# A first MLP group of four tiles with the mean-square work inside it, and the MLP's operands rounded under the output projection's last column

## The chip, the core and the metric

The kernel runs on one core of one Trainium2 chip. The metric is the device time of one execution in microseconds (us), and what is compared is the median of several executions. Each execution of the profile is one run recorded by the hardware profiler. Engines go by short names in rows: PE is TensorE (matmuls; PEld is its weight load), DVE is VectorE, ACT is ScalarE, POOL is GpSimd, SP is the engine that issues most of the transfers, and SPq its queue of transfers.

## What is computed

The program is one step of a decoder layer for a prompt of 1024 tokens and 8 x 4 sample tokens (1056 in all) at a model width of 1024. An input projection feeds three branches (sparse attention, a state space model, attention into a memory), whose gated outputs are joined to 1536 columns. The change lies behind these, in the last three steps:

```python
def merge(x, o_a, o_b, o_c, gb, w_o):
    mixed = jnp.concatenate([o_a, o_b, o_c], axis=-1) * gb
    return x + mixed @ w_o                       # 1056 x 1536 by 1536 x 1024
def ffn(x, g, w1, w2):
    h = rmsnorm(x, g)                            # mean square over 1024, + 1e-6
    return x + jnp.square(jax.nn.relu(h @ w1)) @ w2    # 1024 -> 4096 -> 1024
# and a last rmsnorm(x, final_norm_g)
```

## The kernel before

**Products.** Everything is float32, and a product of two float32 operands is made as three matmuls in TensorE's rounded type fp32r. Each operand is split into its rounded value (`hi`) and the remainder (`lo`), and `mm3` (lines 122 to 124) adds hi x hi, hi x lo and lo x hi into one bank. `split` (line 112 for the rounding, line 118 for the remainder) rounds on ScalarE and subtracts on GpSimd, or on VectorE where it is called with "dve". The tokens are held in three chunks of 352 columns, so a matmul is 128 x 128 weights by 128 x 352.

**Output projection** (`out_proj`). The 1024 outputs are 8 columns `m` of 128. For each column and each of the three chunks, 12 operand tiles `k` are added up: 108 matmuls. The weights of a column come in two halves, `k` 4 to 11 and `k` 0 to 3; the last column takes `k` 0 to 3 first. `residual(m)` loads the rows of `x_prompt` and `x_sample` for the column into a tile `xr` of its own, transposes them on TensorE and lets ScalarE copy them into `acc`. `add` adds the column's three banks to `acc` on VectorE, and squares the sum on ScalarE (tile `sq`), which VectorE adds into the running sum of squares `ms` (its rows read `msb`).

**MLP** (`ffn`). First the operand `h` is split: 24 pieces (8 of the width by 3 chunks), each as `h2hi` on ScalarE (line 1704) and `h2lo` on VectorE (line 1705), scaled by the norm's weight alone. The root of the mean square is left out here: the squared ReLU lets it be taken out of the whole MLP, so `acc` is multiplied by the mean square instead, and the last norm puts that right with `rm`, its reciprocal. The 4096 hidden columns are 32 tiles of 128, in groups. Per tile: weights `w_ff1` (load into one of three `raw` buffers, split into `hi`, `lo`), 72 matmuls, then per chunk a ReLU (ScalarE, tile `rl`, line 1735), a square (VectorE, 1736), a rounding `yh` (ScalarE, 1737) and a remainder `yl` (VectorE, 1738); and the load and split of the tile's second-layer weights `w_ff2` (line 1742, `f2hi` on ScalarE and `f2lo` on GpSimd). After a group, its second layer: for each of 8 outputs and 3 chunks, three matmuls per tile, and one VectorE add into `acc` (line 1761). Before, the groups are 14 of two tiles and one of four.

**The mean square.** After the first group's first layer, `scale_acc` sums `ms` over the partitions with a matmul by ones for each chunk (line 1713), scales the sums on VectorE (`msb`, line 1714) and multiplies the 8 pieces of `acc` by them, four on VectorE and four on GpSimd (line 1717). Behind it TensorE transposes `ms` (line 1752), and VectorE takes the reciprocals `rm` (line 1753). All of this stands ahead of the group's second layer, whose adds go to the scaled `acc`.

**What sets the order.** The program is written against a framework that schedules it: pools give out buffers (a fourth `raw` has to wait for the first's last reader), and each engine's queue is put in order when the program is built, by an estimate of when instructions can start. At run time each engine goes through its queue strictly in order. So a row can stand in another place of a queue than in the source.

## Time and profile before

| what | value |
|---|---|
| median of three runs | 2028.8 us (2024.67 to 2034.67) |
| the profiled execution's own time | 2028.2 us |
| its span, from first to last instruction | 2026.4 us |
| mean granted clock of TensorE over the span | 0.967 |
| TensorE busy | 94% of the span |
| VectorE, ScalarE, GpSimd busy | 57%, 37%, 21% |

The profiled execution lies within the range of the three runs. TensorE is busy nearly throughout, so what other engines do shows in the time only where TensorE waits for them, or where it runs at a lower granted clock (1.00 in a table by stretch is its full level). A timeline row gives the start, the duration (for several instructions the time from the first's start to the last's end), the instruction as output tile <- input tiles, and in brackets how long the engine was idle before it and what ended that.

### The profile page before, as it was taken

Reading aid. Unit: us, or ns where it says so; the run is one execution under the profiler, and the core shown is the slowest. Engines: PE = TensorE matmul, PEld = TensorE weight load, DVE = VectorE, ACT = ScalarE, POOL = GpSimd, SP = SyncE. Lnnn points to the kernel's source line nnn. Section 1 sums busy time; section 2 is a strip of 40 time slices with the busy share of each in tenths; the row PEclk is TensorE's granted clock in tenths of the full one; section 3 lists DMA queues with packets and bytes.
Section 4 is the critical chain, followed back from the end, with each engine's and each line's share of the span. In section 5 each row is a group of like instructions: output and inputs, shape, how many; then the busy total and the mean of one; then the engine's idle time right before and its main releaser. Section 6 shows DMA issues by size and latency. Waiting matters only on the chain.

```text
span 2026.4 us, 33851 instructions
## 1 busy us (share of the span) xinstructions
PE 1912.8 (94%) x13280; PEld 1727.5 (85%) x13280; DVE 1154.9 (57%) x2759; ACT 756.7 (37%) x1696; POOL 434.4 (21%) x281
## 2 busy tenths in 40 slices
PE   8998999999997999999987999799999999999997
PEld 8987889999996665656545999799999999999997
DVE  6387995425536777787653225745554555554535
ACT  6301224226645676667643224122222211122222
POOL 2043431441112211011100122422211211122200
PEclk9998999999997899999996999899999999999999
DMA  7453334563345533232226222211111111111102
GB/s 266 147 138 87 99 92 111 177 214 126 126 129 143 160 96 117 84 106 71 90 93 190 74 70 62 62 51 44 53 53 42 46 49 43 42 43 52 42 1 86
DMA packets 197609, 191.44 MB, mean 94 GB/s; under 512 B 32845, under 2 KB 176966, under 8 KB 196234
## 3 DMA queue, kind: packets, MB, share of 16 engines
q1 hardware_dynamic: 190730, 154.13, 25.5%
q0 software_dynamic: 6720, 35.16, 5.1%
q8 instruction: 104, 1.70, 0.4%
q14 instruction: 55, 0.45, 0.1%
HBM read 155.34 MB, written 38.55 MB: 96 GB/s over the span
## 4 chain that ended last, share of the span: by engine, by line
PE 51%; DMA 2%; DVE 2%; issue 1%; ACT 1%; SPq 0%; DVEq 0%; POOL 0%; ACTq 0%; POOLq 0%
PE fps L122 12%; PE fps L124 12%; PE fps L123 12%; PE ops L122 2%; PE ops L123 2%; PE ops L124 2%; PE O L903 2%; PE T L889 2%; DMA xs<-cache_slc_kv,idx 1%; PE S L838 1%; PE S L835 1%; PE sS L1494 1%; DMA raw<-w_o 1%; DVE acc L1717 0%; PE xps L1651 0%
## 5 line engine op out<-in xcount | busy, mean ns | idle before, releaser
L1761 DVE TENSOR_TENSOR acc<-fps,acc 128x352 f32<-128x352 f32 (+3 forms) x360 | 185.1, 522 | 156.5 <-PE fps L124 156.5
L123 PE MATMUL fps<-h2lo,hi 128*128 128x352 f32 x768 | 248.6, 324 | 2.0 <-DVE h2lo L1705 2.0
L122 PE MATMUL fps<-h2hi,hi 128*128 128x352 f32 x768 | 248.2, 324 | 1.9 <-ACT h2hi L1704 1.9
L123 PE MATMUL fps<-yl,f2hi 128*128 128x352 f32 (+3 forms) x768 | 246.3, 323 | 3.3 <-DVE yl L1738 3.3
L124 PE MATMUL fps<-h2hi,lo 128*128 128x352 f32 x768 | 249.1, 324 | 0.0
L122 PE MATMUL fps<-yh,f2hi 128*128 128x352 f32 (+3 forms) x768 | 242.6, 325 | 6.0 <-DVE rm L1753 6.0
L124 PE MATMUL fps<-yh,f2lo 128*128 128x352 f32 (+3 forms) x768 | 245.9, 323 | 0.0
L1736 DVE TENSOR_TENSOR rl<-rl 128x352 f32<-128x352 f32 x96 | 132.2, 1378 | 146.1 <-ACT rl L1735 146.1
L118 POOL TENSOR_TENSOR lo<-raw,hi 128x1024 fp32r<-128x1024 f32 (+1 forms) x43 | 96.8, 2252 | 359.1 <-ACT hi L112 359.1
L124 PE MATMUL pso<-hhi,wlo 128*128 128x352 f32 x480 | 157.3, 328 | 0.0
L123 PE MATMUL pso<-hlo,whi 128*128 128x352 f32 x480 | 157.3, 328 | 0.0
L122 PE MATMUL pso<-hhi,whi 128*128 128x352 f32 x480 | 157.2, 328 | 0.0
L118 POOL TENSOR_TENSOR f2lo<-raw,f2hi 128x1024 fp32r<-128x1024 f32 x32 | 79.1, 2474 | 361.6 <-ACT f2hi L112 348.5
L843 DVE TENSOR_REDUCE nst<-S 128x1 f32<-128x384 f32 (+4 forms) x264 | 108.9, 433 | 80.2 <-PE S L838 59.5
L122 PEld LDWEIGHTS fps<-yh,f2hi 128*128 128x128 f32 x768 | 144.0, 189 | 7.8 <-DVE rm L1753 6.3
L123 PEld LDWEIGHTS fps<-yl,f2hi 128*128 128x128 f32 x768 | 144.8, 189 | 5.0 <-DVE yl L1738 3.6
L123 PEld LDWEIGHTS fps<-h2lo,hi 128*128 128x128 f32 x768 | 145.4, 189 | 2.3 <-DVE h2lo L1705 2.3
L122 PEld LDWEIGHTS fps<-h2hi,hi 128*128 128x128 f32 x768 | 145.2, 189 | 2.2 <-ACT h2hi L1704 2.2
L124 PEld LDWEIGHTS fps<-h2hi,lo 128*128 128x128 f32 x768 | 146.1, 190 | 0.0
L124 PEld LDWEIGHTS fps<-yh,f2lo 128*128 128x128 f32 x768 | 144.8, 189 | 1.4
L844 ACT ACTIVATE P<-S,nst 128x384 f32<-128x384 f32 (+4 forms) x264 | 127.4, 489 | 33.3 <-DVE nst L843 29.1
L112 ACT ACTIVATE f2hi<-raw 128x1024 fp32r<-128x1024 f32 x32 | 33.8, 1059 | 282.6 <-PE fps L123 268.7
(593 smaller groups left out, 4535.5 us busy)
## 6 DMA issues: line engine op xcount, KB each, us to landing
raw<-w_ff SPq DMA_DIRECT2D x64, 512.0 KB
wraw<-w_in SPq DMA_DIRECT2D x28, 512.0 KB
xs<-cache_mem_kv SPq DMA_DIRECT2D x16, 512.0 KB
s_gb<-st SPq DMA_DIRECT2D x36, 176.0 KB
x<-x_prompt SPq DMA_DIRECT2D x8, 512.0 KB
wraw<-w_mem_kv SPq DMA_DIRECT2D x8, 512.0 KB
qd<-s_q SPq DMA_DIRECT2D x32, 128.0 KB
ngb<-s_gb SPq DMA_DIRECT2D x64, 64.0 KB
```

What stands on the lines that cost most here:

```text
L112: nc.scalar.activation(hi, src, AF.Copy)
L118: eng.tensor_tensor(lo, src, hi.bitcast(F32), op=ALU.subtract)
L122: mm(ps, ahi, bhi, start=start, stop=False)
L123: mm(ps, ahi, blo, start=False, stop=False)
L124: mm(ps, alo, bhi, start=False, stop=stop)
L835: nc.tensor.matmul(S[:, :w], ctx["QA"][:, qs], KA[:, k0:k0 + w], start=True, stop=False)
L843: nc.vector.tensor_reduce(t[:, 0, pi, i:i + 1], S[:, o:o + pw], axis=AX.X, op=ALU.max, negate=True)
L844: nc.scalar.activation(P[:, o:o + pw], S[:, o:o + pw], AF.Exp, bias=t[:, 0, pi, i:i + 1], accum_out=t[:, 1, pi, i:i + 1])
L889: nc.tensor.transpose(T[:w, i * 128:(i + 1) * 128], Ps[i, si][:, o:o + w], self.ident)
L903: nc.tensor.matmul(O[c * 64:(c + 1) * 64, :256], v, pv[:w, c], start=n == 0, stop=n == total - 1)
L1736: tt(r, r, r, op=ALU.mult)
L1761: tt(acc[:, m, o:o + n], ps[:, :n], acc[:, m, o:o + n], op=ALU.add)
```

## The change

Four things are changed.

1. The first group has four tiles (0 to 3) instead of two; the two-tile groups begin at tile 4, and the last four stay.
2. The sums over the partitions, the transposes, the reciprocals and the scaling of `acc` are called after tile 1 of the first group, and tiles 2 and 3 follow.
3. The split of `h` for the widths 0 to 6 (all but the last) is called within the last column of the output projection, after its first half; the pool with the first half's operands (`mixb`) is closed there, and `h2hi` and chunk 0 of `h2lo` are laid into its space. For chunks 1 and 2 only `h2hi` is called there.
4. The residual's rows go into the `raw` buffers and into `rl` instead of a tile of their own, and the squares into `rl`.

```diff
-GROUPS = [(2 * i, 2) for i in range(14)] + [(28, 4)]
+GROUPS = [(0, 4)] + [(2 * i, 2) for i in range(2, 14)] + [(28, 4)]
...
-        with self.pool("acc") as rp, self.pool("wts") as wp:
-            with self.pool("mixb") as pool, self.pool("wop", PSUM) as psp:
+        with self.pool("acc") as rp, self.pool("wts") as wp, ExitStack() as self.fst:
+            with self.pool("wop", PSUM) as psp:
+                mb = ExitStack()
+                pool = mb.enter_context(self.pool("mixb"))
                 self.split(*self.mix_tiles(pool, range(4)), self.mixs[:, 0:4], e_lo="dve")
-                self.out_proj(rp, wp, pool, psp)
+                self.out_proj(rp, wp, pool, psp, mb)
...
         def residual(m):
-            xr = pool.tile([128, 9, 128], F32, name="xr", tag="xr", bufs=1)
-            nc.sync.dma_start(xr[:, 0:8], A["x_prompt"][0][:, cols(m)].rearrange("(i p) c -> p i c", p=128))
-            nc.sync.dma_start(xr[:NS, 8], xsv[:, cols(m)])
+            xr = wp.tile([128, 8, 128], F32, name="raw", tag="raw", bufs=3)
+            nc.sync.dma_start(xr, A["x_prompt"][0][:, cols(m)].rearrange("(i p) c -> p i c", p=128))
+            xrs = rp.tile([128, 512], F32, name="rl", tag="rl", bufs=2)
+            nc.sync.dma_start(xrs[:NS, 0:128], xsv[:, cols(m)])
             for i0 in (0, 4, 8):
                 pt = bank()
                 for i in range(i0, min(i0 + 4, 9)):
                     r = 128 if i < 8 else NS
-                    nc.tensor.transpose(pt[:, (i - i0) * 128:(i - i0) * 128 + r], xr[:r, i], self.ident[:r, :r])
+                    nc.tensor.transpose(pt[:, (i - i0) * 128:(i - i0) * 128 + r], xr[:, i] if i < 8 else xrs[:r, 0:128], self.ident[:r, :r])
...
-                    sq = pool.tile([128, 352], F32, name="sq", tag="sq", bufs=2)
+                    sq = rp.tile([128, 512], F32, name="rl", tag="rl", bufs=2)[:, :n]
...
+                if m == KT - 1 and ks[0] == 0:
+
+                    mb.close()
+                    fh = self.fst.enter_context(self.pool("ffh"))
+                    self.h2hi = fh.tile([128, KT, NT], R32, name="h2hi")
+                    self.h2lo = [fh.tile([128, KT, CHUNKS[0][1]], R32, name="h2lo0")]
+                    for k in range(KT - 1):
+                        self.split2(0, k)
+                    for ci in (1, 2):
+                        for k in range(KT - 1):
+                            self.split2(ci, k, False)
             add(m, pss)
+    def split2(self, ci, k, lo=True):
+
+        nc = self.nc
+        o, n = CHUNKS[ci]
+        src, hi, g = self.acc[:, k, o:o + n], self.h2hi[:, k, o:o + n], self.g2[:, k:k + 1]
+        if lo is not None:
+            nc.scalar.activation(hi, src, AF.Copy, scale=g)
+        if lo or lo is None:
+            nc.vector.scalar_tensor_tensor(self.h2lo[ci][:, k], src, g, hi.bitcast(F32), op0=ALU.mult, op1=ALU.subtract)
...
-            hhi = pool.tile([128, KT, NT], R32, name="h2hi")
-            hlo = [pool.tile([128, KT, n], R32, name=f"h2lo{o}") for o, n in CHUNKS]
-            for ci, (o, n) in enumerate(CHUNKS):
-                cs = slice(o, o + n)
+            hhi, hlo = self.h2hi, self.h2lo
+            hlo += [pool.tile([128, KT, n], R32, name=f"h2lo{o}") for o, n in CHUNKS[1:]]
+            for ci in range(3):
                 for k in range(KT):
-                    nc.scalar.activation(hhi[:, k, cs], acc[:, k, cs], AF.Copy, scale=gg[:, k:k + 1])
-                    stt(hlo[ci][:, k], acc[:, k, cs], gg[:, k:k + 1], hhi[:, k, cs].bitcast(F32), op0=ALU.mult, op1=ALU.subtract)
+                    if ci or k == KT - 1:
+                        self.split2(ci, k, True if k == KT - 1 else None)
...
-            def scale_acc():
+            def sum_ms():
                 for o, n in CHUNKS:
                     cs = slice(o, o + n)
                     ps = psp.tile([128, 512], F32, name="fps", tag="fps", bufs=8)
                     nc.tensor.matmul(ps[:, :n], ones, ms[:, cs], start=True, stop=True)
                     ts(ms[:, cs], ps[:, :n], 1.0 / D, EPS, op0=ALU.mult, op1=ALU.add)
-                for k in range(KT):
-                    eng = nc.gpsimd if k >= 4 else nc.vector
-                    eng.tensor_tensor(acc[:, k], acc[:, k], ms, op=ALU.mult)
...
-                        r = pool.tile([128, 512], F32, name="rl", tag="rl", bufs=2)[:, :n]
+                        r = rp.tile([128, 512], F32, name="rl", tag="rl", bufs=2)[:, :n]
...
-                if g0 == 0:
-                    scale_acc()
-                    for i0 in (0, 8):
-                        pm = psp.tile([128, 512], F32, name="fps", tag="fps", bufs=8)
-                        r = rows(i0)
-                        n = 8 if i0 == 0 else 1
-                        for i in range(i0, i0 + n):
-                            nc.tensor.transpose(pm[:r, (i - i0) * 32:(i - i0) * 32 + 32], ms[0:32, i * 128:i * 128 + r], ident[:32, :32])
-                        nc.vector.reciprocal(rm[:r, i0:i0 + n], pm[:r, 0:n * 32].rearrange("p (i c) -> p i c", c=32)[:, :, 0])
-                        stt(rm2[:r, i0:i0 + n], rm[:r, i0:i0 + n], 1.0 / D, rm[:r, i0:i0 + n], op0=ALU.mult, op1=ALU.mult)
+                    if m == 1:
+                        sum_ms()
+                        for i0 in (0, 8):
+                            pm = psp.tile([128, 512], F32, name="fps", tag="fps", bufs=8)
+                            r = rows(i0)
+                            n = 8 if i0 == 0 else 1
+                            for i in range(i0, i0 + n):
+                                nc.tensor.transpose(pm[:r, (i - i0) * 32:(i - i0) * 32 + 32], ms[0:32, i * 128:i * 128 + r], ident[:32, :32])
+                            nc.vector.reciprocal(rm[:r, i0:i0 + n], pm[:r, 0:n * 32].rearrange("p (i c) -> p i c", c=32)[:, :, 0])
+                            stt(rm2[:r, i0:i0 + n], rm[:r, i0:i0 + n], 1.0 / D, rm[:r, i0:i0 + n], op0=ALU.mult, op1=ALU.mult)
+                        for k in range(KT):
+                            eng = nc.gpsimd if k >= 4 else nc.vector
+                            eng.tensor_tensor(acc[:, k], acc[:, k], ms, op=ALU.mult)
...
-        j = pool.tile([128, 512], F32, name="fj", tag="rl", bufs=2)
+        j = self.rp.tile([128, 512], F32, name="rl", tag="rl", bufs=2)
```

The queues below are in the order in which the engines work them off; line numbers of the changed kernel are its own (1713 and 1715 are the split of `h`, 1666 and 1667 the squares and their sum, 1755 to 1758 the MLP's ReLU, square, rounding and remainder).

ScalarE from the end of the output projection to the first group's first ReLU, before (`hi` and `f2hi` are weights, `sq` a square of the residual sum):

```order
L112 ACTIVATE hi<-raw 128x1024
L1663 ACTIVATE sq<-acc 128x352
L1704 ACTIVATE h2hi<-acc,g2c 128x352 x24
L112 ACTIVATE f2hi<-raw 128x1024 x2
L1735 ACTIVATE rl<-fps 128x352 x2
L1737 ACTIVATE yh<-rl 128x352 x2
L112 ACTIVATE hi<-raw 128x1024
L1735 ACTIVATE rl<-fps 128x352 x2
L112 ACTIVATE f2hi<-raw 128x1024
```

The same stretch in the changed kernel:

```order
L112 ACTIVATE hi<-raw 128x1024
L1713 ACTIVATE h2hi<-acc,g2c 128x352 x21
L1666 ACTIVATE rl<-acc 128x352
L1713 ACTIVATE h2hi<-acc,g2c 128x352
L1666 ACTIVATE rl<-acc 128x352
L1713 ACTIVATE h2hi<-acc,g2c 128x352
L112 ACTIVATE hi<-raw 128x1024
L112 ACTIVATE f2hi<-raw 128x1024 x2
L1713 ACTIVATE h2hi<-acc,g2c 128x352
L1666 ACTIVATE rl<-acc 128x352
L112 ACTIVATE f2hi<-raw 128x1024
L1755 ACTIVATE rl<-fps 128x352 x2
```

Twenty-one `h2hi` now follow the split of the first MLP weights directly and stand ahead of the last column's squares; ahead of the first ReLU stand three `f2hi` instead of two, the third being that of the group's third tile.

VectorE from the last column's adds to the MLP's first squares, before (one `h2lo` tile for each chunk):

```order
L1658 TENSOR_TENSOR acc<-ops,acc 128x352
L1664 TENSOR_TENSOR msb<-msb,sq 128x352
L1658 TENSOR_TENSOR acc<-ops,acc 128x352
L1664 TENSOR_TENSOR msb<-msb,sq 128x352
L1707 MEMSET ones 128x128
L1705 SCALAR_TENSOR_TENSOR h2lo_14208<-acc,g2c,h2hi 128x352 x8
L1705 SCALAR_TENSOR_TENSOR h2lo_14209<-acc,g2c,h2hi 128x352 x8
L1705 SCALAR_TENSOR_TENSOR h2lo_14210<-acc,g2c,h2hi 128x352 x8
L1736 TENSOR_TENSOR rl<-rl 128x352 x2
L1738 TENSOR_TENSOR yl<-rl,yh 128x352 x2
```

The same stretch in the changed kernel (tiles 14119, 14248 and 14249 are `h2lo` of chunks 0, 1 and 2; `msb<-msb,rl` adds a square into the sum):

```order
L1715 SCALAR_TENSOR_TENSOR h2lo_14119<-acc,g2c,h2hi 128x352 x5
L1661 TENSOR_TENSOR acc<-ops,acc 128x352
L1715 SCALAR_TENSOR_TENSOR h2lo_14119<-acc,g2c,h2hi 128x352 x2
L1661 TENSOR_TENSOR acc<-ops,acc 128x352 x2
L1715 SCALAR_TENSOR_TENSOR h2lo_14248<-acc,g2c,h2hi 128x352 x7
L1715 SCALAR_TENSOR_TENSOR h2lo_14249<-acc,g2c,h2hi 128x352 x3
L1667 TENSOR_TENSOR msb<-msb,rl 128x352
L1715 SCALAR_TENSOR_TENSOR h2lo_14249<-acc,g2c,h2hi 128x352 x3
L1715 SCALAR_TENSOR_TENSOR h2lo_14119<-acc,g2c,h2hi 128x352
L1667 TENSOR_TENSOR msb<-msb,rl 128x352
L1715 SCALAR_TENSOR_TENSOR h2lo_14248<-acc,g2c,h2hi 128x352
L1715 SCALAR_TENSOR_TENSOR h2lo_14249<-acc,g2c,h2hi 128x352
```

Seven `h2lo` of chunk 0 now stand between the last column's adds, seven of chunk 1 follow the last add, and the sums of squares stand among those of chunk 2.

TensorE from the end of the second tile's matmuls to what follows the mean square's sums and transposes, before:

```order
L124 MATMUL fps<-h2hi,lo 128x352
L1713 MATMUL fps<-msb,ones 128x352 x3
L1752 MATMUL fps<-ident,msb 128x32 x8
L1752 MATMUL fps<-ident,msb 32x32
L122 MATMUL fps<-yh,f2hi 128x352
L123 MATMUL fps<-yl,f2hi 128x352
L124 MATMUL fps<-yh,f2lo 128x352
```

The same stretch in the changed kernel:

```order
L124 MATMUL fps<-h2hi,lo 128x352
L1736 MATMUL fps<-msb,ones 128x352 x3
L1772 MATMUL fps<-ident,msb 128x32 x8
L1772 MATMUL fps<-ident,msb 32x32
L122 MATMUL fps<-h2hi,hi 128x352
L123 MATMUL fps<-h2lo_14119,hi 128x352
L124 MATMUL fps<-h2hi,lo 128x352
```

Behind the transposes of `msb` stands the third tile's first layer instead of the second layer.

## Rows read from the trace of the kernel before

**Rows 1.** The page: busy time, share of the span and instructions of each engine.
```profile
PE 1912.8 (94%) x13280; PEld 1727.5 (85%) x13280; DVE 1154.9 (57%) x2759; ACT 756.7 (37%) x1696; POOL 434.4 (21%) x281
```

**Rows 2.** Table by stretch: us, busy PE, PEld, DVE, ACT, POOL (instructions), clock, DMA share, GB/s.
```profile
1200.00:1220.00 20.00, 20.00 (x128) 19.72 (x127) 3.64 (x6) 4.28 (x8) 3.69 (x2) 1.00 0.28 80
...
1251.20:1257.20 6.00, 5.99 (x21) 6.00 (x22) 6.00 (x13) 6.00 (x13) 0.00 (x0) 0.52 0.32 87
...
1290.30:1296.20 5.90, 0.00 (x0) 0.00 (x0) 5.90 (x5) 0.00 (x0) 4.69 (x2) 0.57 0.00 0
...
1296.20:1301.40 5.20, 5.12 (x17) 5.13 (x18) 3.73 (x12) 0.00 (x0) 0.00 (x0) 0.50 0.00 0
```

**Rows 3.** TensorE's waits, 1195 to 1330: us in total, times, longest.
```profile
PE fps L122 <- DVE rm L1753: 6.0, 1, 6.0
...
PE fps L123 <- DVE yl L1738: 3.3, 1, 3.3
...
PE fps L123 <- DVE h2lo L1705: 2.0, 1, 2.0
...
PE fps L122 <- ACT h2hi L1704: 1.9, 1, 1.9
...
PE fps L1752 <- DVE msb L1714: 1.1, 1, 1.1
```

**Rows 4.** Timeline of TensorE: start, duration, instruction [idle before and releaser].
```profile
1246.51 0.32 PE L124 MATMUL ops<-mxh,lo 128*128 128x352 f32 x1
...
1276.93 1.94 PE L1713 MATMUL fps<-msb,ones 128*128 128x352 f32 x6
...
1280.70 0.43 PE L122 MATMUL fps<-yh,f2hi 128*128 128x352 f32 x1
...
1296.28 0.66 PE L122 MATMUL fps<-yh,f2hi 128*128 128x352 f32 x1 [5.99 <-DVE rm L1753]
```

**Rows 5.** Timeline of ScalarE around the MLP's start.
```profile
1235.24 1.06 ACT L112 ACTIVATE hi<-raw 128x1024 fp32r<-128x1024 f32 x1 [1.96 <-PE ops L123]
...
1248.11 11.61 ACT L1704 ACTIVATE h2hi<-acc,g2c 128x352 fp32r<-128x352 f32 x24
...
1261.52 0.44 ACT L1735 ACTIVATE rl<-fps 128x352 f32<-128x352 f32 x1
```

**Rows 6.** Timeline of GpSimd (first row) and VectorE around the MLP's start.
```profile
1247.89 2.36 POOL L118 TENSOR_TENSOR lo<-raw,hi 128x1024 fp32r<-128x1024 f32 x1 [16.10 <-ACT hi L112]
...
1248.23 2.40 DVE L1664 TENSOR_TENSOR msb<-msb,sq 128x352 f32<-128x352 f32 x1 [0.84 <-ACT sq L1663]
...
1250.69 11.86 DVE L1705 SCALAR_TENSOR_TENSOR h2lo<-acc,g2c,h2hi 128x352 fp32r<-128x352 f32 x24
...
1276.16 0.53 DVE L1738 TENSOR_TENSOR yl<-rl,yh 128x352 fp32r<-128x352 f32 x1 [0.56 <-ACT yh L1737]
...
1280.36 6.32 DVE L1717 TENSOR_TENSOR acc<-acc,msb 128x1056 f32<-128x1056 f32 x2
```

**Rows 7.** Timelines of GpSimd and VectorE where both ask for work at once.
```profile
251.29 2.90 POOL L118 TENSOR_TENSOR wlo<-wraw,whi 128x1024 fp32r<-128x1024 f32 x1 [8.34 <-ACT whi L112]
...
251.87 2.86 DVE L1251 TENSOR_TENSOR tB<-GT,E 128x512 f32<-128x512 f32 x1
...
1260.74 4.53 POOL L118 TENSOR_TENSOR f2lo<-raw,f2hi 128x1024 fp32r<-128x1024 f32 x1 [10.49 <-ACT f2hi L112]
...
1262.48 0.51 DVE L1736 TENSOR_TENSOR rl<-rl 128x352 f32<-128x352 f32 x1
```

**Rows 8.** Timelines: issue of an MLP weight load on SP, ScalarE's split that waits for it.
```profile
1319.12 0.33 SPq L1742 DMA_DIRECT2D raw<-w_ff  x1
...
1322.58 1.06 ACT L112 ACTIVATE f2hi<-raw 128x1024 fp32r<-128x1024 f32 x1 [1.02 <-DMA raw<-w_ff]
```

**Rows 9.** Timelines of SP and TensorE: the load of the residual's rows, and its transposes.
```profile
1098.21 0.39 SPq L1645 DMA_DIRECT2D xr<-x_prompt  x1
...
1103.16 1.07 PE L1651 MATMUL xps<-ident,xr 128*128 128x128 f32 x8 [1.03 <-DMA xr<-x_prompt]
```

More of the change, by code (lines that the diff above doesn't have):

```diff
@@ L228, in run @@
             ck.close()
-            self.ffn(wp)
+            self.ffn(rp, wp)
     def column(self, pool, psp, src, k, tag):
@@ L1626, in weights, with out_proj @@
         return hi, lo
-    def out_proj(self, rp, wp, pool, psp):
+    def out_proj(self, rp, wp, pool, psp, mb):
         nc, A = self.nc, self.A
@@ L1690, in out_proj @@
                         product(pss, (hi[:, k - ks[0]], lo[:, k - ks[0]]), k, ci, k == halves[0][0], k == halves[1][-1])
-            add(m, pss)
-    def ffn(self, wp):
+                if m == KT - 1 and ks[0] == 0:
[8 more added lines that the diff above has]
+                            self.split2(ci, k, False)
@@ L1694, in ffn @@
+            add(m, pss)
+    def split2(self, ci, k, lo=True):
[6 more added lines that the diff above has]
+            nc.vector.scalar_tensor_tensor(self.h2lo[ci][:, k], src, g, hi.bitcast(F32), op0=ALU.mult, op1=ALU.subtract)
+    def ffn(self, rp, wp):
         nc, A = self.nc, self.A
@@ L1695, in ffn @@
         tt, ts, stt = nc.vector.tensor_tensor, nc.vector.tensor_scalar, nc.vector.scalar_tensor_tensor
-        ident, acc, ms, gg = self.ident, self.acc, self.ms, self.g2
+        ident, acc, ms, self.rp = self.ident, self.acc, self.ms, rp
         rows = lambda i: 128 if i < 8 else NS
         with self.pool("ff") as pool, self.pool("ffp", PSUM) as psp:
-            hhi = pool.tile([128, KT, NT], R32, name="h2hi")
-            hlo = [pool.tile([128, KT, n], R32, name=f"h2lo{o}") for o, n in CHUNKS]
-            for ci, (o, n) in enumerate(CHUNKS):
-                cs = slice(o, o + n)
+            hhi, hlo = self.h2hi, self.h2lo
+            hlo += [pool.tile([128, KT, n], R32, name=f"h2lo{o}") for o, n in CHUNKS[1:]]
+            for ci in range(3):
```

## The prediction

> **What bounds the kernel now.** TensorE is busy for 94% of the span [rows 1], so a change pays only where TensorE stands still or runs at its lower clock. I first looked for such places around the start of the MLP. In the output projection's steady stretch 128 matmuls take 20.00 us at granted clock 1.00 [rows 2], 0.158 us each with the two cut records at the edges left out; that is the full level, 2.4 GHz. The MLP starts where the projection's last matmul ends, 1246.51 + 0.16 = 1246.67 [rows 4].
>
> From there I count what TensorE loses, by matmuls against the clock on the wall:
> - Entry. Two tiles of the first layer are 2 x 3 x 8 x 3 = 144 matmuls, 22.75 us at 0.158. They end at 1276.93, when the mean-square sum starts [rows 4]: 30.26 us, so 7.5 are lost. The waits named are ScalarE's rounding (`h2hi` 1.9) and VectorE's remainder (`h2lo` 2.0) [rows 3]; the rest is the granted clock, 0.52 in the 6.00 us behind them [rows 2], the lower level.
> - The sums and their transposes take 1276.93 to 1280.70 = 3.8 us [rows 4], of which 1.1 is a wait for VectorE's `msb` [rows 3]; 2.7 is work that stays.
> - Second layer of that group: 3.3 us for the last `yl`, 6.0 for `rm` [rows 3], and then 17 matmuls in 5.2 us at clock 0.50 [rows 2], which at 0.158 were 2.7: 2.5 lost. Together 11.8. The reason is VectorE: the scaling of `acc` by the mean square starts at 1280.36 [rows 6], and TensorE resumes at 1296.28 [rows 4], 15.9 us later, with `yl` and the reciprocals queued inside it.
> Sum: 7.5 + 1.1 + 11.8 = 20.4 us, 1.0% of the 2026.4 us span. This is all that the change can take there.
>
> **The change, part by part.** The profiled execution took 2028.2 us, its span 2026.4; the median of the three runs is 2028.8, so I make the sum against 2028.2 and add 0.6.
>
> *Rounding moved under the last column.* The order fences show ScalarE doing 21 of the 24 `h2hi` right after the split of the first MLP weights, which ends at 1235.24 + 1.06 = 1236.3 [rows 5]. At 11.61 / 24 = 0.484 each they end at 1246.4, in time for TensorE at 1246.67. Seven `h2lo` of chunk 0 are done by then too (11.86 / 24 = 0.495 each [rows 6], VectorE has nothing else but one add). So TensorE starts at once, and the entry wait of 1.9 + 2.0 and its clock loss are gone: +7.5 if nothing is late next. The cover is the upper half of the last column, 72 matmuls or 11.4 us, against 10.2 us of ScalarE.
>
> *What is late next.* Behind the 21 stand two squares, two `h2hi`, and the split of tile 1's weights: about 1.9 + 1.0 us, so GpSimd can start its half of that split (`lo`) at 1249.3. VectorE then runs one unbroken row of two-input instructions from 1247.3 on (seven `h2lo`, three more, the `msb` add, four `h2lo`, an add ...), and these two engines exclude each other: a GpSimd split that takes 2.36 us alone [rows 6] took 4.53 when it was asked for at 1260.74 during such a row, and ran only after the TENSOR_TENSOR that followed the `h2lo` had ended at 1262.99, 2.28 us before its own end; behind a TENSOR_TENSOR at 251.29 it went in next, and VectorE's `tB` waited for it (2.86 us) [rows 7]. So I let GpSimd in at each TENSOR_TENSOR and not between `h2lo`: the first `msb` add ends at 1247.3 + 10 x 0.495 + 0.5 = 1252.8, tile 1's `lo` at 1255.0 (TensorE wants it at about 1255.3); the second add ends at 1257.4, and `f2lo` of tile 0 at 1259.7. The remaining `h2lo` come some 1.5 us late for TensorE, which reaches the sums at 1246.7 + 22.75 + 1.5 = 1271 and has done them at 1273.
>
> *The head of ScalarE's queue.* Now the split `f2hi` of the third tile's second-layer weights stands ahead of the first ReLU (order fence). Its buffer is one of three `raw`, free only when `f2lo` of tile 0 is done: load issued at 1259.7. Such a load, issued at 1319.12, let a waiting split go at 1322.58 [rows 8], 3.5 us. So f2hi starts at 1263.2, and the first ReLU at 1264.3; before it was at 1261.52 [rows 5], with TensorE then 5 us further behind. All of VectorE's MLP work hangs on that ReLU.
>
> *Sums between tile 1 and tile 2.* TensorE's transposes of `msb` wait for VectorE's scaling of the sums, which is queued behind five ReLU-square-remainder pieces. Before, the first ReLU to the end of the fifth `yl` was 1261.52 to 1276.16 + 0.53 [rows 5, 6]: 15.2 us, with four GpSimd splits pressed in. I count three or four now and take 14.5, then 3.5 for the three scalings with one square and one split between them: 18 us. So the transposes end at 1264.3 + 18 = 1282.3, not at 1272.1 (1246.67 + 22.75 + 2.7): 10.2 lost, and a gap of this length was followed by the low clock each time (granted 0.57 inside the 6.0 us gap, 0.50 behind it [rows 2]): 2.5 more. Together 12.7.
>
> *The 15.9 us of scaling* then lie beside tiles 2 and 3: 144 matmuls, 22.75 + 2.5 us, from 1282.3 to 1307.6. VectorE is free at 1282.3 + 15.9 = 1298.2, and four pieces of square and remainder (0.5 + 0.6 of waiting + 0.5 each) give the `yl` that the second layer needs first at about 1305, or 1307 with one more GpSimd split. TensorE asks for it at 1307.6 + 9 x 0.158 = 1309. So the 11.8 are gone; if that margin of 2 us were not there, each late us would cost one.
>
> *Group of four.* The matmuls are as many. VectorE has 24 adds fewer, worth nothing while TensorE waits for none of them.
>
> *Residual rows in the `raw` buffers.* Three of them now carry three loads per column instead of two. The row loads of a column still come a column ahead. The x_prompt rows of column 1 are loaded before the sample stage ends, so the wait of 1.03 us at 1103.16 [rows 9] goes. The x_sample rows are issued later; see the rivals. I take +1.0 (bounds 0 and 1.0: another load could take its place).
>
> Sum: 20.4 - 12.7 + 1.0 = 8.7 us. 2028.2 - 8.7 + 0.6 = **2020.1**; I say 2020. The bounds of the unknown: the ReLU chain is 18 us, but 15 if no split is pressed in (-3.0), and 21 if every VectorE instruction waits for one (+3.0). With the residual's 1.0 that leaves 2017 to 2024.
>
> *A rule against the row.* On [rows 7] a GpSimd split asked for at 1260.74 waited 2.2 us, over four VectorE instructions. The Trainium skill, "SBUF — State Buffer", section "SBUF: two separate sides", says that the pair of ports that the two engines share is locked for one whole instruction, by whichever starts first. By that rule the split would have gone in at the next instruction's end, and no split starves in the new row; the row shows otherwise, so I keep the starving rival.
>
> **The rivals.**
> 1. *The ReLU is not held up* (0.20). If GpSimd goes in at once, `lo` ends at 1251.7, `f2lo` at 1254.1, and the ReLU starts at 1258.7; TensorE loses 4.6 + 2.5. Gain 13.3 + 1.0: 2014.5, or 2012 if the chain is short too. For it: the split at 1247.89 did go in at once, VectorE's add waiting [rows 6]. Against: that one was asked for in a gap of VectorE.
> 2. *GpSimd starves for the whole row* (0.14). `lo` then runs from 1257.5, `f2lo` ends at 1262.1, the ReLU starts at 1266.7: 2.4 us later than in the forecast, 2022.5. TensorE also waits some 4.5 us for `lo` at 1255.3, but that is inside the later wait. For it: [rows 7], 1260.74. Against: 251.29.
> 3. *The x_sample rows come late: slower* (0.08). In the order of the changed kernel TensorE transposes them, in each of six columns, 26 matmuls after the eight big transposes, so 1.07 [rows 9] + 26 x 0.158 = 5.2 us after the column starts. SP issues their load only after the `msb` add of the column before, near the column's start. A load of 3.5 us [rows 8] is in time; one that took 5.0 from 1098.21 to 1103.16 [rows 9] barely is. Each us over 5.2 costs 6 us, and a gap of 2 us also the clock, 2.5 a column: at 7.2 us of landing 6 x (2 + 2.5) = 27, and 2047. It decides from about 6.7 us of landing on, where it eats 8.7.
> 4. *The early rounding is not early* (0.05). `h2hi` lies where the first half's operands lay; if its writes waited for the whole column, entry loss and a later ReLU would leave 2027 to 2030.
>
> **How the numbers follow.** The forecast has 0.50, the rivals 0.20, 0.14, 0.08, 0.05, and 0.03 is left for what I don't see (slower). A measurement of this kernel can tell about 0.5%, 10.1 us, from no change; the bound is 2018.7. The forecast lies 1.4 us above it, so of its 0.50 I give 0.22 to faster and 0.28 to the same. Faster: 0.22 + 0.20 = 0.42. Same: 0.28 + 0.14 + 0.05 = 0.47. Slower: 0.08 + 0.03 = 0.11. The range takes in the first two rivals: 2012 to 2025, and leaves out 0.2.
>
> **What would show it.** Right: the first matmul on `h2hi` follows the projection without a gap; ScalarE's `f2hi` waits for a `raw<-w_ff` load ahead of its first ReLU; TensorE waits 5 to 10 us in the transposes of `msb`, with granted clock near 0.5 behind; no wait for `yl` or `rm` at the second layer. Wrong: transposes that wait under 2 us (rival 1), waits for the residual's transposes in every column (rival 3), or a wait for `yl` at about 1309 of the old time.

## The result and the profile after

The changed kernel takes 2012.58 us in the median of 10 runs (2007.08 to 2021.96); the kernel before took 2029.16 us in 10 runs. The ratio is 0.9921, with a 95% interval of 0.9901 to 0.9940: 16.6 us less, and 12 to 20 by the interval. The prediction said 2020.

Each ratio below is taken against runs of the kernel before made beside that kernel's own (their medians lie between 2024.5 and 2029.2 us), so the times of different rows are not to be subtracted from each other; the changed kernel's second set of runs has 2010.52 against 2024.47 us, 14.0 less. The spread within a kernel is as wide as the effect, so I compare two stretches that every profile shows. **A** runs from the prompt attention's last matmul to the output projection's last, **B** from there to TensorE's last instruction. What lies ahead of A moves by some 9 us between profiles, though its program is the same in all kernels here.

| kernel | A, us | B, us | ratio to before | 95% interval |
|---|---|---|---|---|
| before (two profiles) | 194.0, 192.6 | 768.5, 768.0 | 1 | |
| changed (two profiles) | 187.5, 190.2 | 758.1, 758.1 | 0.9921 and 0.9927 | 0.9901 to 0.9940, 0.9901 to 0.9953 |
| front_only | 189.8 | 769.3 | 0.9984 | 0.9967 to 1.0001 |
| groups_of_two | 187.5 | 767.7 | 0.9990 | 0.9975 to 1.0005 |
| no_early | 188.0 | 758.2 | 0.9929 | 0.9904 to 0.9954 |
| late_round | 190.3 | 766.9 | 0.9981 | 0.9963 to 1.0000 |
| late_round_2 | 190.4 | 762.8 | 0.9957 | 0.9937 to 0.9978 |
| w2_late | 189.0 | 754.8 | 0.9920 | 0.9897 to 0.9943 |
| w2_late_lo_dve | 189.6 | 754.4 | 0.9908 | 0.9886 to 0.9930 |
| late_transposes | 188.9 | 756.8 | 0.9925 | 0.9897 to 0.9953 |
| scale_last | 187.3 | 749.5 | 0.9894 | 0.9866 to 0.9922 |
| scale_last_dve | 188.7 | 747.9 | 0.9893 | 0.9864 to 0.9921 |

One of late_round's twelve runs took 3652.72 us and is left out.

The change takes 768.3 - 758.1 = 10.2 us from B. A is 193.3 in the mean of before and 188.9 in the mean of the twelve profiles that have the residual's rows in the `raw` buffers: 4.4 us. Together 14.6; the 2.0 that are left of the 16.6 lie within the interval.

Now the rows of after. The page's first part, to be held against [rows 1]:

```profile
PE 1903.6 (95%) x13280; PEld 1721.1 (86%) x13280; DVE 1146.6 (57%) x2735; ACT 754.2 (38%) x1696; POOL 434.2 (22%) x281
```

VectorE has 24 adds fewer (2759 to 2735). TensorE's waits from 1180 to 1320 (us in total, times, longest):

```profile
PE fps L123 <- DVE h2lo L1715: 3.6, 2, 1.8
PE fps L1772 <- DVE msb L1737: 2.4, 1, 2.4
```

Of the five waits in [rows 3] the two large ones (`rm`, `yl`) and that for `h2hi` are gone, `h2lo` has grown from 2.0 to 3.6, `msb` from 1.1 to 2.4. TensorE's timeline at the places of [rows 4]:

```profile
1236.16 0.32 PE L122 MATMUL fps<-h2hi,hi 128*128 128x352 f32 x1
...
1265.12 1.94 PE L1736 MATMUL fps<-msb,ones 128*128 128x352 f32 x6
1267.04 0.71 PE L1772 MATMUL fps<-ident,msb 32*128 32x32 f32 x5
1270.14 0.40 PE L1772 MATMUL fps<-ident,msb 32*128 32x32 f32 x4 [2.39 <-DVE msb L1737]
...
1295.26 0.32 PE L122 MATMUL fps<-yh,f2hi 128*128 128x352 f32 x1
```

The MLP starts without a gap, at 1236.16. The sums start 29.0 us later (before 30.3), the transposes end at 1270.5, 34.4 us after the start, and the second layer starts at 59.1 us without a wait. Four tiles and the mean square need 4 x 11.38 + 2.7 = 48.2 us at the full clock, by the prediction's 0.158 us a matmul: 10.9 of the 20.4 us that were lost in the MLP's head are still lost.

ScalarE, GpSimd and VectorE in the same place, the counterparts of [rows 5, 6]:

```profile
1225.70 10.18 ACT L1713 ACTIVATE h2hi<-acc,g2c 128x352 fp32r<-128x352 f32 x21
...
1248.68 0.50 ACT L1666 ACTIVATE rl<-acc 128x352 f32<-128x352 f32 x1 [7.74 <-DVE msb L1667]
1249.08 1.04 ACT L112 ACTIVATE f2hi<-raw 128x1024 fp32r<-128x1024 f32 x1
1253.12 0.46 ACT L1755 ACTIVATE rl<-fps 128x352 f32<-128x352 f32 x1 [2.99 <-PE fps L124]
```

```profile
1238.64 2.50 POOL L118 TENSOR_TENSOR lo<-raw,hi 128x1024 fp32r<-128x1024 f32 x1 [17.35 <-ACT hi L112]
1241.09 5.25 POOL L118 TENSOR_TENSOR f2lo<-raw,f2hi 128x1024 fp32r<-128x1024 f32 x2
1250.20 3.12 POOL L118 TENSOR_TENSOR f2lo<-raw,f2hi 128x1024 fp32r<-128x1024 f32 x1 [3.86 <-DVE h2lo L1715]
```

```profile
1236.80 11.41 DVE L1715 SCALAR_TENSOR_TENSOR h2lo<-acc,g2c,h2hi 128x352 fp32r<-128x352 f32 x10
...
1238.78 2.74 DVE L1715 SCALAR_TENSOR_TENSOR h2lo<-acc,g2c,h2hi 128x352 fp32r<-128x352 f32 x1
...
1248.13 0.51 DVE L1667 TENSOR_TENSOR msb<-msb,rl 128x352 f32<-128x352 f32 x1
```

Three GpSimd splits went in between `h2lo` instructions, the first as soon as it was asked for and the other two each behind one `h2lo`; the second VectorE row is one of these ten `h2lo`, the one that waited for the first split. The fourth split, at 1250.20, was let in only behind the `msb` add that followed the `h2lo` in progress (the add at 1250.55 took 0.52 us, the `h2lo` behind it 2.72). Ten `h2lo` that take 10 x 0.495 = 5.0 us by [rows 6] took 11.4: the 6.5 us are GpSimd's. The `h2lo` come late to TensorE, and the `msb` add behind them comes late to ScalarE, whose third square waits 7.7 us for a free `rl` buffer. The granted clock around TensorE's waits (us, busy PE, PEld, DVE, ACT, POOL with instructions, clock, DMA share, GB/s); the first stretch holds the two waits for `h2lo`, the third lies behind the one for `msb`:

```profile
1242.00:1248.00 6.00, 2.43 (x10) 1.85 (x10) 6.00 (x5) 0.00 (x0) 4.34 (x2) 0.90 0.66 184
1248.00:1254.00 6.00, 6.00 (x32) 5.83 (x31) 6.00 (x9) 1.91 (x3) 3.12 (x1) 0.82 0.27 79
...
1271.00:1277.00 6.00, 6.00 (x30) 6.00 (x30) 6.00 (x3) 0.46 (x1) 6.00 (x2) 0.74 0.26 77
1277.00:1283.00 6.00, 6.00 (x39) 6.00 (x38) 6.00 (x3) 0.00 (x0) 6.00 (x3) 1.00 0.00 0
```

Behind the waits TensorE runs partly at its lower level, as behind the gap in [rows 2]: 32 and 30 matmuls in 6 us, with granted clocks of 0.82 and 0.74, where 39 are counted at 1.00.

### The profile page after: what moved, and what is told of

Read it like the earlier page. It is cut to its first block, busy times and chain, and to the rows that moved or that the text cites. A ratio compares the mean times of both kernels' runs of the same rounds, so it can differ in the third digit from the quotient of the medians.

```text
span 2005.5 us, 33835 instructions
## 1 busy us (share of the span) xinstructions
PE 1903.6 (95%) x13280; PEld 1721.1 (86%) x13280; DVE 1146.6 (57%) x2735; ACT 754.2 (38%) x1696; POOL 434.2 (22%) x281
## 4 chain that ended last, share of the span: by engine, by line
PE 50%; DVE 2%; DMA 1%; ACT 1%; issue 1%; DVEq 0%; SPq 0%; POOL 0%; ACTq 0%; POOLq 0%
PE fps L122 12%; PE fps L124 12%; PE fps L123 12%; PE ops L124 2%; PE ops L122 2%; PE ops L123 2%; PE O L905 2%; PE T L891 2%; DMA xs<-cache_slc_kv,idx 1%; DVE h2lo L1715 1%; PE S L840 1%; PE S L837 1%; PE sS L1496 1%; PE xps L1654 0%; PE fps L1801 0%
## 5 line engine op out<-in xcount | busy, mean ns | idle before, releaser
L1784 DVE TENSOR_TENSOR acc<-fps,acc 128x352 f32<-128x352 f32 (+3 forms) x336 | 173.5, 523 | 167.5 <-PE fps L124 167.5
L1756 DVE TENSOR_TENSOR rl<-rl 128x352 f32<-128x352 f32 x96 | 126.2, 1315 | 136.8 <-ACT rl L1755 136.8
```

Source lines behind the costliest of these rows:

```text
L1756: tt(r, r, r, op=ALU.mult)
L1784: tt(acc[:, m, o:o + n], ps[:, :n], acc[:, m, o:o + n], op=ALU.add)
```

## Experiments

**The changed kernel once more** (no edit).

> The changed kernel once more, for a second profile. In its first profile TensorE reaches the MLP 10.5 us earlier than in the kernel before (of that 4.0 arose before the last prompt block ends, 5.5 from there to the end of the projection's third transposes, 1.0 at the residual's load), and the MLP itself is 10.4 us shorter. Theory A: the 6.5 us between the end of the prompt attention and the first columns belong to the change (the order of loads on SP's queue), the 4.0 ahead of that are chance: the second profile again shows the MLP's first matmul 6 to 7 us earlier, counted from the end of the prompt attention, and the MLP 10 us shorter; time 2011 to 2015. Theory B: both are chance of the gathers and only 1.0 is the change's: the second profile shows 1 to 3 us there.

Measured: 2010.52 us (6 runs), ratio 0.9927. B is 758.1 to a tenth, and the second profile has the same 3.6 and 2.4 us of waits. A is 190.2, 3 us under before and not 6.5. **The kernel before once more** settles what is chance in A:

> The kernel before once more, for a second profile of the stretch between the end of the prompt attention's last block and the MLP. In its first profile that stretch took 194.0 us; in the five profiles with the residual's rows in the raw buffers it took 187.5, 190.2, 189.8, 188.0 and 187.5. If the change gives 6 us there: 193 to 195 again. If the first profile was slow there by chance and only the 1.0 of the residual's wait is the change's: 188 to 191. The MLP from the projection's end to the last matmul: 768 to 769 in either case.

Measured: 2027.14 us in its one run, A 192.6, B 768.0. The two of before are at 192.6 and 194.0, the twelve others between 187.3 and 190.4. They do not overlap; the gain in A is 4.4 us in the means, with only two profiles of before, and lies between what the two theories said.

**The fourth part alone**, on the kernel before:

```diff
-            xr = pool.tile([128, 9, 128], F32, name="xr", tag="xr", bufs=1)
...
+            xr = wp.tile([128, 8, 128], F32, name="raw", tag="raw", bufs=3)
...
+            xrs = rp.tile([128, 512], F32, name="rl", tag="rl", bufs=2)
...
-                    sq = pool.tile([128, 352], F32, name="sq", tag="sq", bufs=2)
+                    sq = rp.tile([128, 512], F32, name="rl", tag="rl", bufs=2)[:, :n]
```

> The kernel before with only the fourth part of the change: the residual's rows in the raw buffers and in rl, the squares in rl. Groups, mean square and rounding stay as before. Theory A (the order of SP's loads gives 6.5 us): 2022 to 2024. Theory B (it gives the 1.0 us of the one wait and nothing else): 2027 to 2029. If the x_sample rows came late in six columns, over 2030.

Measured: 2023.16 us (12 runs), ratio 0.9984. The interval, 0.9967 to 1.0001, is 6.7 us less to 0.2 more and does not part the theories; the profile does: A is 189.8, as in the changed kernel, with nothing else of the change in it. What goes is seen in TensorE's waits at the end of the sample stage, before:

```profile
PE sS L1563 <- DMA xs<-cache_mem_kv: 6.6, 2, 4.1
PE sS L1567 <- ACT KTs L1343: 4.8, 4, 2.6
PE sS L1567 <- DVE KTs L1345: 3.8, 4, 1.2
```

and in front_only:

```profile
PE sS L1563 <- DMA xs<-cache_mem_kv: 5.4, 2, 2.8
PE sS L1567 <- DVE KTs L1345: 4.4, 4, 1.7
PE sS L1567 <- ACT KTs L1343: 2.8, 4, 0.7
```

The memory's keys (`KTs`) are copied out of banks by ScalarE and VectorE in turn. Before, a rounding (`mxh`) of the projection's own operand, which waited for its load, stood ahead of ScalarE's last such copy. ScalarE's and TensorE's timelines at this place before, then in front_only:

```profile
1079.65 1.06 ACT L112 ACTIVATE mxh<-mxr 128x1024 fp32r<-128x1024 f32 x1 [5.25 <-DMA mxr<-s_mix]
1080.61 0.58 ACT L1343 ACTIVATE KTs<-sS 128x512 f32<-128x512 f32 x1
...
1081.24 0.65 PE L1567 MATMUL sS<-KTs,Qm 128*32 128x128 f32 x8 [2.60 <-ACT KTs L1343]
```

```profile
1076.26 0.60 ACT L1343 ACTIVATE KTs<-sS 128x512 f32<-128x512 f32 x1 [4.33 <-PE sS L1563]
1077.38 1.06 ACT L112 ACTIVATE mxh<-mxr 128x1024 fp32r<-128x1024 f32 x1 [0.52 <-DMA mxr<-s_mix]
...
1076.91 0.66 PE L1567 MATMUL sS<-KTs,Qm 128*32 128x128 f32 x8 [0.74 <-ACT KTs L1343]
```

The copy now stands first and waits for TensorE alone. All twelve profiles with this part have the wait for ScalarE's `KTs` at 2.8 or 2.9, both profiles of before have 4.8: 2.0 of the 4.4 us. The 1.0 of the residual's load [rows 9] is gone. The wait for the cache loads is 3.8 to 6.3 (5.1 in the mean) against 6.6 and 6.8, while that for VectorE's `KTs` rose from 3.8 to between 4.0 and 6.3 (4.5 in the mean). All of TensorE's waits in A add up to 21.6 and 21.9 before and to 18.1 in the mean of the twelve, so they show 3.7 of the 4.4 us.

**The early rounding undone, a failed attempt.** The block with `split2` was moved from the last column to the end of the projection:

```diff
-                    for k in range(KT - 1):
-                        self.split2(0, k)
...
+                    self.split2(ci, k)
```

> The changed kernel with all 24 roundings h2hi and remainders h2lo behind the output projection, as before the change; the group of four and the mean square inside it stay. Theory A: GpSimd's splits go in at once and push VectorE's row back, so the first remainders done early bring the ReLU chain no earlier, and the chain (some 17 us from the first ReLU to the end of the transposes) sets the time: loss in the MLP's head 10 to 12 us as in the changed kernel, 2012 to 2015. Theory B: the early rounding is worth the 7.5 us that TensorE lost at the entry before: 2019 to 2021.

Measured: 2012.73 us (6 runs), B 758.2. This is no evidence for theory A: the queues are the same as in the changed kernel, 21 `h2hi` right behind the first weights' split. The scheduler puts them there by itself. As I read it, `h2hi` lies where the first half's operands lay, and once these are read nothing holds it back; no run has the buffers' place alone. The call's place does nothing. To hold the rounding back it needs data that come late, so this is added to the edit above:

```diff
+            gl = pool.tile([128, KT], F32, name="g2l")
+            stt(gl, acc[:, KT - 1, NT - KT:NT], 0.0, self.g2, op0=ALU.mult, op1=ALU.add)
+            self.g2 = gl
```

> The changed kernel with the rounding really held back: the norm's weight by which it scales is first passed through a tiny VectorE instruction that reads the last sum of the last column, so that no h2hi can start ahead of the projection's end (in the kernel no_early the scheduler had put the 21 roundings back under the last column, and its MLP was the same 758.2 us). Group of four, mean square and residual stay. ScalarE's queue now has three weight splits ahead of the 24 h2hi. Theory A: early rounding is worth little, since VectorE's row of h2lo then runs after GpSimd's splits instead of being interrupted by them, and ends at about the same time (18 us after the projection): the MLP 758 to 761 us, time 2011 to 2015. Theory B: it is worth the 7.5 us lost at the entry before: the MLP 765 us or more, time 2018 to 2022.

Measured: 2020.74 us (11 runs), B 766.9, as theory B wanted, but by another way than it said: the second layer starts 64.0 us after the projection's end, 4.9 later than in the changed kernel, and the other 3.9 us come evenly over the rest of the MLP, where nothing waits. GpSimd does stay out of VectorE's row in this kernel, as the prediction's rule has it: a split that was asked for at 1258.08 let nine `h2lo`, the one in progress among them, and a TENSOR_TENSOR go ahead of it (the second row below is the eight of these `h2lo` that began after that):

```profile
1258.08 6.83 POOL L118 TENSOR_TENSOR f2lo<-raw,f2hi 128x1024 fp32r<-128x1024 f32 x1 [7.16 <-ACT f2hi L112]
...
1258.17 4.05 DVE L1708 SCALAR_TENSOR_TENSOR h2lo<-acc,g2l,h2hi 128x352 fp32r<-128x352 f32 x8
1262.13 0.52 DVE L1751 TENSOR_TENSOR rl<-rl 128x352 f32<-128x352 f32 x1
```

The slower rest of the MLP asked for a second version with every tile where it was (the edit is shown against late_round; all queues are the same in both):

```diff
-            gl = pool.tile([128, KT], F32, name="g2l")
...
+            stt(rm2[:, 0:KT], acc[:, KT - 1, NT - KT:NT], 0.0, self.g2, op0=ALU.mult, op1=ALU.add)
+            self.g2 = rm2
```

> As late_round, with the same queues, but the held-back weight lies in a tile that the kernel has anyway (rm2, which is written over later), so that every other tile keeps the place that it has in the changed kernel. In late_round the MLP was 8.8 us longer than in the changed kernel; 4.9 of them lay ahead of the second layer, and 3.9 came evenly over the rest of the MLP, where a matmul followed the one before after 0.1609 us instead of 0.1599. Theory A (the slower pitch came from the 32 bytes by which the new tile shifted the others): the pitch is 0.1599 again, the MLP 763 us, time 2015 to 2019; the early rounding with a group of four is then worth 4.9 us. Theory B (the pitch was that execution's or the chip's, or comes from the late rounding itself): 0.1609 or some other value, the MLP 765 to 768, time 2018 to 2023.

Measured: 2018.52 us (11 runs), B 762.8, and the second layer starts at 63.9 us. The rest of the MLP is as fast as in the changed kernel again. Late_round and late_round_2 between 1500 and 1700:

```profile
1500.00:1700.00 200.00, 200.00 (x1245) 200.00 (x1244) 101.95 (x152) 43.24 (x73) 41.93 (x18) 1.00 0.16 48
```

```profile
1500.00:1700.00 200.00, 200.00 (x1253) 200.00 (x1252) 102.24 (x152) 44.48 (x74) 43.17 (x18) 1.00 0.16 48
```

At the same clock of 1.00, 1253 matmuls instead of 1245 in 200 us. So early rounding is worth 762.8 - 758.1 = 4.7 us beside a group of four, some 2 us of which are the three weight splits that late rounding leaves ahead of `h2hi` on ScalarE (its wait is 3.8, where before, with one split ahead, it was 1.9 [rows 3]); what is left for the early rounding itself is then, as an estimate, 2.7:

```profile
PE fps L122 <- ACT h2hi L1706: 3.8, 1, 3.8
PE fps L123 <- DVE h2lo L1708: 3.6, 2, 2.2
PE fps L1766 <- DVE msb L1726: 2.1, 1, 2.1
```

**The groups of before**, with all else of the change:

```diff
-GROUPS = [(0, 4)] + [(2 * i, 2) for i in range(2, 14)] + [(28, 4)]
+GROUPS = [(2 * i, 2) for i in range(14)] + [(28, 4)]
```

> The changed kernel with the groups of before (14 of two tiles, one of four), so that the mean square's scaling again stands directly ahead of the first second layer. Early rounding and residual in the raw buffers stay. Theory A: the 11.8 us that TensorE lost there before (3.3 for yl, 6.0 for rm, 2.5 of clock) come back, less the 2.0 us of clock that the changed kernel loses in the third tile: 2021 to 2024. Theory B: the group of four only moves the wait, and the time stays within 3 us of the changed kernel's.

Measured: 2023.36 us (12 runs), ratio 0.9990, B 767.7: the group of four is worth 9.6 us, and without it nothing that can be measured is left of the change in B. TensorE's waits:

```profile
PE fps L122 <- DVE rm L1773: 6.0, 1, 6.0
PE fps L123 <- DVE h2lo L1715: 3.6, 2, 1.8
PE fps L1772 <- DVE msb L1737: 2.1, 1, 2.1
PE fps L123 <- DVE yl L1758: 1.7, 1, 1.7
```

Theory A: the waits for `rm` and `yl` are back, the latter with 1.7 us instead of the 3.3 of before. The four kernels make a square. B without either part is 768.0 to 769.3; with early rounding alone 767.7; with the group of four alone 762.8; with both 758.1. Early rounding gains 0.3 to 1.6 where VectorE's scaling stands ahead of the second layer and eats what is won, 4.7 where it doesn't (with the 2 us of ScalarE's order in them).

**The second-layer weights late.** The next four runs go after the 10.9 us that are left. First the loads and splits of `w_ff2` of the first group are called behind the fourth tile:

```diff
-                    self.split(hi2, lo2, raw2)
-                    hid.append((yh, yl, hi2, lo2))
+                    def second(mc=mc, yh=yh, yl=yl):
...
+                    late.append(second)
+                    if m >= 3:
+                        while late:
+                            late.pop(0)()
```

> The changed kernel, but the loads and splits of the first group's second-layer weights are called behind the fourth tile instead of behind each tile, so that GpSimd has one split and not three in VectorE's row of h2lo. Theory A (these splits, 5.2 us of GpSimd at once, cost TensorE the 3.6 us of waits for h2lo and the 2 us or so of lower clock behind them): h2lo waits under 1.5 us, the MLP 751 to 755, time 2004 to 2009. Theory B (the splits must run somewhere, and now stand in the ReLU chain): the wait for msb grows by as much, the MLP 757 to 760, time 2010 to 2014.

Measured: 2009.84 us (6 runs), B 754.8. With one GpSimd split in it instead of three, the same row of ten `h2lo` takes 7.19 us instead of 11.41:

```profile
1242.12 7.19 DVE L1715 SCALAR_TENSOR_TENSOR h2lo<-acc,g2c,h2hi 128x352 fp32r<-128x352 f32 x10
```

```profile
PE fps L1777 <- DVE msb L1737: 3.4, 2, 1.8
PE fps L123 <- DVE h2lo L1715: 1.3, 1, 1.3
```

Both theories have a share: 3.3 us are gained, and 1.0 of what `h2lo` gave went into `msb`. Then also tile 1's remainder goes to VectorE:

```diff
-                    hi, lo = self.weights(wp, A["w_ff1"][0][:, mc], KT, "dve" if m == 0 else "pool")
+                    hi, lo = self.weights(wp, A["w_ff1"][0][:, mc], KT, "dve" if m < 2 else "pool")
```

> As w2_late, and the remainder of tile 1's first-layer weights is made on VectorE (1.2 us) instead of GpSimd (2.5 us in which VectorE stands), so that no GpSimd split is left in the row of h2lo. Theory A: no wait for h2lo over 0.5 us, the wait for msb under 1.5, full clock to the third tile, the MLP 748 to 751, time 2002 to 2006. Theory B (the ReLU chain sets the end of the transposes whatever runs ahead of it): 756 to 759, time 2010 to 2013.

Measured: 2008.25 us (6 runs), B 754.4. The wait for `h2lo` is gone, but `msb` still costs 2.8, and a wait of 1.1 for `yh` appears at the second layer. Neither theory: what is won ahead comes back as other waits for VectorE.

**The transposes behind the second layer**, in the changed kernel:

```diff
+                    if g0 == 0 and si == 23:
+                        for i0 in (0, 8):
...
```

> The changed kernel with one thing moved: the nine transposes of ms and the reciprocals behind them come after the first group's second layer, so that nothing on TensorE waits for VectorE's scaling of the sums (msb). The sums and the scaling of acc stay behind tile 1. Theory A (the 2.4 us of wait for msb and some 2 us of lower clock behind it are lost for good): the MLP 753 to 755 us instead of 758.1, time 2007 to 2010. Theory B (VectorE's work ahead of the second layer is the bound, and the wait moves to yl of the fourth tile): a wait for yh or yl of 2 to 5 us at the second layer, the MLP 757 to 758.5, time 2011 to 2014.

Measured: 2012.23 us (6 runs), B 756.8. The second layer starts 5.2 us earlier, at 53.9, but 1.3 us are left at the end. TensorE's waits:

```profile
PE fps L123 <- DVE h2lo L1715: 3.6, 2, 1.9
PE fps L122 <- ACT yh L1757: 2.1, 2, 1.2
```

Theory B: the wait moved to the fourth tile's `yh`, behind VectorE's and GpSimd's scaling of `acc`. So the scaling itself has to leave the first layer. **The sums behind the fourth tile, the scaling on VectorE alone, one piece ahead of each output**, with the weights and transposes late:

```diff
-                    if m == 1:
+                    if m == 3:
...
-                            eng = nc.gpsimd if k >= 4 else nc.vector
-                            eng.tensor_tensor(acc[:, k], acc[:, k], ms, op=ALU.mult)
+                    if g0 == 0 and o == 0:
+                        nc.vector.tensor_tensor(acc[:, m], acc[:, m], ms, op=ALU.mult)
```

> As late_transposes, with the sums and the scaling of acc behind tile 4 (the scaling on VectorE alone, one piece ahead of each output of the second layer) and the first group's second-layer weights called late as in w2_late. GpSimd keeps its splits. Theory A (with the scaling out of the first layer, VectorE has room, and the eight banks let TensorE run ahead of the adds): only the wait of 1.3 for h2lo is left, the MLP 748 to 751, time 2001 to 2005. Theory B (the eight scalings, 11 us, now stand ahead of the first adds, and TensorE runs out of banks): a wait for a bank of 3 to 8 us in the second layer, 753 to 757, time 2007 to 2011.

Measured: 2003.28 us (6 runs), B 749.5; one wait of 1.3 us for `h2lo` is all that is left, and no bank runs out. Theory A. The last 1.3, **with VectorE making all remainders of the first group's weights**:

```diff
-                    hi, lo = self.weights(wp, A["w_ff1"][0][:, mc], KT, "dve" if m == 0 else "pool")
+                    hi, lo = self.weights(wp, A["w_ff1"][0][:, mc], KT, "dve" if m < 4 else "pool")
...
-                        self.split(hi2, lo2, raw2)
+                        self.split(hi2, lo2, raw2, e_lo="dve" if g0 == 0 else "pool")
```

> As scale_last, and all splits of the first group's weights have their remainder made on VectorE (1.2 us) instead of GpSimd (2.4 us, in which VectorE stands). Theory A (what a GpSimd split costs VectorE is twice what VectorE needs itself): no wait for h2lo, no wait ahead of the second layer, the MLP 747 to 749, time 2000 to 2003, 1 to 2 us under scale_last. Theory B (the seven remainders, 8.6 us more on VectorE's own queue, delay its ReLU pieces): waits for yl or lo of over 1 us, the MLP as long as in scale_last or longer.

Measured: 2006.03 us (6 runs), B 747.9, no wait at all: theory A by B, though the time lies 3 us above the 2000 to 2003 that it named. The same ten `h2lo`, now without any split among them, take 5.04 us:

```profile
1247.42 5.04 DVE L1715 SCALAR_TENSOR_TENSOR h2lo<-acc,g2c,h2hi 128x352 fp32r<-128x352 f32 x10
...
1260.64 1.23 DVE L118 TENSOR_TENSOR lo<-raw,hi 128x1024 fp32r<-128x1024 f32 x1 [0.42 <-ACT hi L112]
```

The second row is one of the remainders that VectorE now makes itself. The whole first layer of the group and the sums, as one stretch:

```profile
1246.80:1294.60 47.80, 47.80 (x295) 47.27 (x295) 32.07 (x53) 21.73 (x38) 2.69 (x2) 1.00 0.29 91
```

TensorE is busy for 47.80 of 47.80 us at clock 1.00. B is 768.3 - 747.9 = 20.4 us shorter than before, as much as the loss that was counted in the kernel before. The last two kernels can't be told apart in time (0.9894 and 0.9893); in B they are 8.6 and 10.2 us shorter than the changed kernel.

## Why the prediction was right and where it was not

The sign and the range held (2012 to 2025, measured 2012.58 at its very end), and so did the outline in the MLP: the start without a gap, and no wait for `yl` or `rm`. The two other signs that the prediction named did not show: no `f2hi` waited for a load ahead of the first ReLU, and the transposes waited 2.4 us and not 5 to 10. 8.7 us of gain were forecast and 16.6 measured. By its steps:

- **The loss of 20.4 us before.** Right, but for a price read a little low: 0.158 us a matmul, where the MLP's matmuls start every 0.1599 us at clock 1.00 (the changed kernel's profile, 1450 to 1900). With 0.1599 the loss before is 20.1 us, and 10.3 of it are left in the changed kernel instead of 10.9. scale_last_dve shortened B by 20.4, and nothing was left to wait for.
- **Entry.** The start without a gap came as said. "+7.5 if nothing is late next" was the wrong half: the sums started only 1.3 us earlier than before. The step that failed is the rule read from [rows 7], that GpSimd is let in at a TENSOR_TENSOR and not between `h2lo`. In the changed kernel three splits went in between `h2lo`. The page "SBUF — State Buffer" of the Trainium skill says (section "SBUF: two separate sides") that whichever engine starts first has the shared pair of ports for one whole instruction; the rows at 1238.64 and 1241.09 agree with it, and the `h2lo` at 1238.78 took 2.74 us while the split ran. The first rival had this, but took from it only that the splits end early, and not that VectorE's row ends 6.5 us late. Yet the prediction's rule is not wrong everywhere. The changed kernel's fourth split (1250.20) passed by the end of an `h2lo` and went in behind the `msb` add, and in late_round a split stayed out for nine `h2lo` and took 6.83 us, so there the split did not go in at the next instruction's end. What decides it is not shown.
- **The head of ScalarE's queue.** The first ReLU started 17.0 us after the projection's end; 17.6 was forecast, for the wrong reason, so that the two agree is luck. Nothing waited for a `w_ff2` load. ScalarE waited 7.7 us for an `rl` buffer, because the squares now share two buffers and the `msb` add that frees one stands behind ten `h2lo`; then the ReLU waited 3.0 for TensorE, itself late by `h2lo`.
- **The chain from the first ReLU to the end of the transposes.** Forecast 18, measured 1270.5 - 1253.1 = 17.4. The transposes ended 34.4 us after the projection (forecast 35.6), and the lower clock behind took 24.7 - 22.75 = 2.0 (forecast 2.5). The loss of 12.7 was forecast; it is 10.9, cut into 3.6 of `h2lo`, 2.4 of `msb` and the clock behind each, where the forecast had one gap of 5 to 10 us.
- **Scaling beside tiles 2 and 3.** Right: no wait for `yl` or `rm`, the second layer starts at once. The group of four carries it (9.6 us by groups_of_two).
- **24 adds fewer are worth nothing.** No run has them alone. The head accounts for 20.1 - 10.3 = 9.8 of the 10.2 us in B (with 0.1599 us a matmul); what the other 0.4 are I did not find.
- **Residual.** +1.0 was forecast, 4.4 measured: the largest mis-sized term. I followed the moved loads to the residual and no further. The change of buffers also put ScalarE's queue in another order, with the sample stage's copy ahead of the operand's rounding; the 2.0 us of `KTs` that this gave back were in the trace of before, and the shorter wait for the cache loads came on top.
- **Second rival.** GpSimd did not starve for the whole row in the changed kernel. **Third rival.** The x_sample rows were not late in any column. **Fourth rival**: no; the writes of `h2hi` did not wait.

## What to carry to other kernels

- A gain at one place of a chain is real only if the next wait in the chain is gone too: early rounding gave 0.3 to 1.6 us beside groups of two, and 4.7 beside a group of four, some 2 of them by the order on ScalarE. Test two parts of a change in all four combinations.
- Where GpSimd helps VectorE with work that both can do, count what it takes away: here ten `h2lo` took 5.04, 7.19 and 11.41 us with none, one and three GpSimd splits among them, over 2 us a split, and VectorE needed 1.2 for a split itself. When VectorE's row is the one that others wait for, move such work off, later, or onto VectorE.
- A scheduler that orders by readiness makes the place of a call mean little (no_early has every queue of the changed kernel); what held the work back was data that come late (late_round). After a change of buffers look at every queue they touch, also in the stage ahead.

## What the runs showed of the hardware

- A tile of 32 bytes per partition ahead of the MLP's operands made the following matmuls follow one another after 0.1609 us instead of 0.1599, at granted clock 1.00 and with no waits (late_round against late_round_2): 3.9 us over the MLP. It is one profile of each, but the other twelve profiles all have 0.1598 or 0.1599, three of them from the chip that ran late_round; the medians, 2020.74 and 2018.52, lie the same way, but their spread would hide as much. Which operand's place does it was not tried.
- GpSimd's splits and VectorE's two-input instructions held each other up for whole instructions, and who came first was not the same everywhere, though it was the same in both profiles of before and in both of the changed kernel. `lo` was let in between two `h2lo` (1238.64, 2.50 us). An `f2lo` asked for while no other split ran waited until a TENSOR_TENSOR behind the `h2lo` had ended: the one at 1260.74 before took 4.53 us [rows 7], the one at 1250.20 after 3.12, the one at 1258.08 in late_round 6.83. Why stays open.
